# Attention stage of a one-core encoder trunk: TensorE's order written from a clock model, three block lanes, and two pieces of work given to GpSimd

## The chip, the core and the metric

The kernel runs on one core of one Trainium2 chip. The time is the device time of one execution in microseconds (us). The kernel before takes 3174.94 us, the median of three runs (3173.12 to 3175.65).

A core has five engines that run at the same time, each with its own queue of instructions in a fixed order. TensorE (PE in the profile; its weight loads are listed apart as PEld) multiplies matrices into the PSUM banks. VectorE (DVE) and ScalarE (ACT) read those banks and do the elementwise work. GpSimd (POOL) does elementwise work between SBUF tiles. SyncE (SP) issues most of the transfers.

## The reference, cut to what matters

The program is a trunk of two layers over 1024 positions of width 1024. Layer 0 mixes with two recurrent head groups and layer 1 with attention; each layer goes on with a squared-ReLU MLP and a gated embedding. The change is in the attention mixer of layer 1, 16 heads of width 64. Each chunk of 64 positions sees itself and the 8 chunks before it:

```python
qkv = (h @ w_qkv).reshape(bsz, seq, 3, C_HEADS, C_HEAD_DIM)
q = rmsnorm(qkv[:, :, 0], q_g) * (C_HEAD_DIM ** -0.5)
k = rmsnorm(qkv[:, :, 1], k_g)
v = qkv[:, :, 2]
...
s = jnp.einsum('bqhd,bkhd->bhqk', q_c, k_b).astype(jnp.float32) + bias
...
prob = jax.nn.softmax(s, -1).astype(v.dtype)
return jnp.einsum('bhqk,bkhd->bqhd', prob, v_b)
...
mix = chunk_band_attention(h, ...) @ attn_w_out[o]
x = x + mix
```

The bias is looked up by head and clipped relative distance.

## The kernel before

Positions lie in eight tiles of 128, and the 16 heads in 8 pairs. A matrix product in near-fp32 precision is made from three products of split operands (`mm3`, L305: high by high, high by low, low by high).

The attention stage is `layer1_in` (L1619). It has 16 steps, each a head pair `pr` and one half `hf` of the positions (four position tiles). A step has three parts, and a fourth piece of work stands beside them:

- **Input products**, `attn_in` (L1709): for each of the four position tiles 24 matmuls of 384 columns (q, k and v of two heads at once) into a bank with the tag `dense`; ScalarE copies q and k out, scaled (L1742), ScalarE and VectorE split v (L1746, L1747). Then the norms: GpSimd squares (L1754), VectorE sums (L1755), `rsqrt_small` (L280) makes 1/sqrt by three rounds of three small VectorE instructions (L287 to L289) and VectorE multiplies q and k by it (L1758, 128x1024). The weights of a pair are loaded by three transfers and split by ScalarE and VectorE (`load_qkv`, L1699, L1705, L1706).
- **Norm and layout**, `attn_norm` (L1761): four TensorE transposes for k and four for q into a `dense` bank; from there ScalarE writes the high parts (L1780), a second copy of the query at the other 64 partitions (L1782), and VectorE the low parts (L1783).
- **Four blocks** (two heads by two pairs of position tiles), `attn_block` (L1788): for each of its two tiles near scores into a bank `sn` and far scores into a bank `sf`; VectorE adds the bias table `toep` and takes the maximum in one instruction (L1838), ScalarE makes the exponentials (L1848, L1851) and scales by 1/sum (L1855). Then TensorE transposes the probabilities `pb` into banks `pt`, ScalarE and VectorE split them into `ptile` (L347, L348 in `split_scaled`), and TensorE multiplies by v into the bank `o` (`po`).
- **Filler**, the end of `attn_ins` (L1640): when the 16 steps' products are out, the products of the gated embedding (`ple_proj`, L1531) and the first part of the output projection (`out_early`, L1560).

PSUM has eight banks here: two `dense`, two `sn`, one `sf`, two `pt`, one `o`.

What sets the order. `run` (L128) is a small planner at build time: each part is a Python generator ("lane"), `self.now` is a time counted from the matmuls written so far (`mm` L165, `tr` L188), a lane that yields a name is not taken up again until `LAT[name]` microseconds later (a table, L35), one that yields a key waits until another lane has marked it, and the first lane in the list that is due is taken. Two lanes run `attn_block`, then come `attn_norms` and `attn_ins`. `attn_ins` may be three steps ahead of the finished ones (`("at", s - 3)`), `attn_norms` two. What the planner writes down is the program order. It isn't the final order: the whole program stands in

```python
with tile.TileContext(nc, schedule_with_timeline_sim=True) as tc:
```

so the framework's scheduler orders each engine's instructions anew, from the program order as a priority and a timeline that it simulates. The bias table of a head is prepared on GpSimd (L1796, L1797) in the head's first block.

Of the kernel before, what the change touches and what calls it, by code (L numbers as in the profile page):

```python
# [82 lines left out]
    "attn_norm0": 0.24,  # L83
    "attn_block0": 0.97,
    "attn_block1": 4.45,
    "attn_block2": 0.43,
    "attn_block3": 0.94,
    "qk": 11.25,
    "norm": 1.28,
# [17 lines left out]

class Trunk:
    def __init__(self, ctx, tc, a, dbg=None, stop=None):
        self.ctx, self.tc, self.nc, self.a = ctx, tc, tc.nc, a  # L110
        self.dbg, self.stop = dbg or {}, stop

        self.now, self.done, self.lat = 0.0, {}, LAT
        self.nd, self.rx, self.late, self.extra = -1, None, None, []

        self.steps, self.begun = [], None

# [10 lines left out]
    def run(self, lanes, ahead=()):  # L128
        state, self.done = [[g, 0.0, None] for g in lanes], {}
        ahead, self.steps = [lanes[n] for n in ahead], []  # L130
        waited = set()
        while state:
            best = None
            for st in state:
# [10 lines left out]
            self.begun, start = None, self.now  # L145
            try:
# [3 lines left out]
                continue  # L150
            if best[0] in ahead and self.begun is not None:
# [4 lines left out]
            if isinstance(r, tuple):  # L156
                best[2] = r
                waited.add(id(best[0]))
            else:
                best[1] = self.now + self.lat.get(r, 0.0)  # L160

    def mark(self, key, after=0.0):
        self.done[key] = self.now + after

    def mm(self, out, lhsT, rhs, start, stop):  # L165
# [5 lines left out]
        if rhs.dtype == F32:  # L171
# [16 lines left out]
    def tr(self, out, in_, ident):  # L188
        self.now += 0.107
# [90 lines left out]
    def rsqrt_small(self, out, x, shape, tag):  # L280
# [5 lines left out]
        for _ in range(3):  # L286
# [1244 lines left out]
    def ple_proj(self, i, pt, acc, scratch, sqt, load_w):  # L1531
# [9 lines left out]
        for n4 in range(2):  # L1541
            hi, lo = load_w(a["w_ple"][i, n4])
            for e in range(4):
                n = 4 * n4 + e
                t = scratch(n)
                for hf in range(2):
                    ps = self.bank()
# [12 lines left out]
    def out_early(self, i, xsrc, pair, xt, load_w, keys):  # L1560
# [36 lines left out]
        if i == 0:  # L1597
            raw = self.wr.tile([P, T], F32, tag="wraw", name="wraw")
            nc.sync.dma_start(out=raw, in_=a["w_out0"][2])
            self.w_next = self.split_w(raw, T, [self.pre.tile([P, T], F32R, tag=f"p{q}", name="w" + q) for q in "hl"])  # L1600
        self.first = [self.bank() for _ in ws]
# [17 lines left out]
    def layer1_in(self):  # L1619
        nc, tc, a = self.nc, self.tc, self.a  # L1620
        with ExitStack() as es:
# [16 lines left out]
            self.run([self.attn_lane(steps, jobs, l1, rbl) for _ in range(2)] + [self.attn_norms(steps, l1), self.attn_ins(steps, l1)])  # L1638

    def attn_ins(self, steps, l1):  # L1640
        kv = {}
        for s, (pr, hf) in enumerate(steps):
# [3 lines left out]
            self.mark(("qk", s), self.lat["qk"])  # L1646
# [29 lines left out]
    def attn_norms(self, steps, l1):  # L1676
        K = []
        for s, (pr, hf) in enumerate(steps):
            yield ("qk", s)
            if s >= 2:  # L1680
                yield ("at", s - 2)
            yield from self.attn_norm(s, self.st[s], l1)
# [3 lines left out]
            self.mark(("in", s), self.lat["norm"])  # L1686

    def attn_lane(self, steps, jobs, l1, rbl):

        for s, h, b in jobs:  # L1690
            yield ("in", s)
            yield from self.attn_block(s, *steps[s], h, b, l1, rbl)
# [16 lines left out]
    def attn_in(self, pr, hf, l1, kv):  # L1709
# [18 lines left out]
        for e in range(4):  # L1728
            i = 4 * hf + e
            ps = self.bank([P, 3, P])  # L1730
# [26 lines left out]
        self.rsqrt_small(nn, ss, [P, 16], "q")  # L1757
        V.tensor_tensor(q4, q4, nn.rearrange("p (n o) -> p n o", o=1).broadcast_to((P, 16, 64)), op=ALU.mult)  # L1758
        return dict(kv, qk=qk)

    def attn_norm(self, s, st, l1):  # L1761
# [5 lines left out]
        for j, g, nm in ((1, self.vec("kg"), "k"), (0, self.dv["qg8"], "Q")):  # L1767
            pt = self.bank()
# [10 lines left out]
            for h, r, o in ((0, h0, h1), (1, h1, h0)):  # L1779
                nc.scalar.activation(F[r, h], pt[r], AF.Copy, scale=g[r])  # L1780
                if not j:
                    nc.scalar.activation(F[o, h], pt[r], AF.Copy, scale=g[r])  # L1782
# [3 lines left out]
            yield "attn_norm0"  # L1786

    def attn_block(self, s, pr, hf, h, blk, l1, rbl):  # L1788
# [5 lines left out]
        if hf == 0 and blk == 0:  # L1794
            t = st["toep"][h]
            G.tensor_scalar(t, t, rbl[:, 2 * pr + h:2 * pr + h + 1], None, op0=ALU.subtract)  # L1796
# [201 lines left out]
```

## Time and profile before

| | |
|---|---|
| median of three runs | 3174.94 us (3173.12 to 3175.65) |
| the profiled execution | 3175.69 us, its span 3174.0 us |
| mean granted TensorE clock | 0.973 |
| input products of the stage, first and last matmul start | 1735.6 and 2255.1 us |
| last product into `po` starts | 2370.7 us |
| `toep` preparation on GpSimd, x16 | median 1297 ns |

The span runs from the first to the last instruction of the profiled execution; the execution's own time is 1.69 us more. The page gives the busy time of each engine, then groups of instructions: their line, engine, operation, what they write and read, how many, the busy time and the mean duration, and the idle time of the engine just before them with what ended it. The windows view gives busy times between two moments of the span, "(x...)" being numbers of instructions, then the granted TensorE clock and the transfers' share.

### The profile page before, as it was taken

To read this page: it belongs to the slowest core of one execution; us is meant where nothing else is said; L and a number is where in the kernel's file an instruction comes from. 1 tells how busy PE (TensorE), PEld (TensorE's weight loads), DVE (VectorE), ACT (ScalarE), POOL (GpSimd) and SP (SyncE) were. 2 spreads that over 40 slices of the span, in tenths; PEclk is the share of its full clock that TensorE was granted. 3 is DMA by queue.
4 is the path that set the end of the run, shared out by engine and by line. 5 is a ranking of instruction groups with operands and counts; after the bars stand their busy time and mean duration, and the time that the engine had idled before them with its cause. 6 is when DMAs were issued, how large, how long until landed. Compare 5 with 4: busy or idle time off the path is not lost.

```text
span 3174.0 us, 46034 instructions
## 1 busy us (share of the span) xinstructions
PE 3057.5 (96%) x17576; PEld 2523.9 (80%) x17576; DVE 2018.1 (64%) x4020; ACT 1387.8 (44%) x2640; POOL 536.1 (17%) x978
## 2 busy tenths in 40 slices
PE   7999999999999999999999989999999999999999
PEld 5777777777778888888887888888788888888887
DVE  6546666567849666655556576776769666655552
ACT  4323433333427554311223577777757555312221
POOL 6524443444500000000005111110200000000002
PEclk8989999999999999999999999999999999999999
DMA  3212112112345333522213100110255332522213
GB/s 128 77 48 64 50 43 85 54 57 64 126 153 209 136 120 112 190 93 100 99 54 129 58 32 33 47 39 16 76 197 205 136 120 107 199 93 93 107 47 106
DMA packets 144716, 309.60 MB, mean 98 GB/s; under 512 B 40944, under 2 KB 43120, under 8 KB 144496
## 3 DMA queue, kind: packets, MB, share of 16 engines
q1 hardware_dynamic: 126064, 273.10, 25.1%
q10 hardware_dynamic: 18432, 33.56, 2.7%
q8 instruction: 138, 2.26, 0.3%
q14 instruction: 82, 0.67, 0.1%
HBM read 232.16 MB, written 74.45 MB: 97 GB/s over the span
## 4 chain that ended last, share of the span: by engine, by line
PE 79%; DVE 10%; ACT 4%; DMA 4%; issue 2%; POOL 1%; SPq 0%; DVEq 0%; POOLq 0%; ACTq 0%
PE dps L175 67%; PE ch L175 2%; PE po L175 1%; PE pm L175 1%; PE iz L175 1%; PE tp L175 1%; DVE ptile L348 1%; PE pt L190 1%; DVE f L1056 1%; DMA wraw<-in_w_out 1%; PE sn L175 1%; DMA wraw<-in_w_qkv 1%; DVE wlo L302 1%; DVE pb L1838 1%; POOL subt L413 1%
## 5 line engine op out<-in xcount | busy, mean ns | idle before, releaser
L175 PE MATMUL dps<-r,act 128*128 128x512 f32 x3528 | 824.4, 392 | 0.0
L175 PEld LDWEIGHTS dps<-r,act 128*128 128x128 f32 x3528 | 662.2, 188 | 145.6
L175 PE MATMUL dps<-xg,whi 128*128 128x512 f32 x1280 | 437.9, 423 | 16.2 <-ACT xg L350 7.1
L175 PE MATMUL dps<-late,act 128*128 128x512 f32 x1536 | 352.9, 391 | 0.0
L175 PEld LDWEIGHTS dps<-late,act 128*128 128x128 f32 x1536 | 288.5, 188 | 63.1
L1495 POOL TENSOR_TENSOR pn<-pn,prs 128x512 f32<-128x512 f32 x32 | 47.1, 1475 | 1621.3 <-ACT prs L384 1527.3
L175 PE MATMUL dps<-wq,act 128*128 128x384 f32 x1536 | 304.8, 343 | 8.0 <-DVE vs L1747 4.2
L175 PEld LDWEIGHTS dps<-xg,whi 128*128 128x128 f32 x1280 | 237.2, 197 | 67.0 <-ACT xg L350 7.1
L175 PEld LDWEIGHTS dps<-wq,act 128*128 128x128 f32 x1536 | 264.5, 190 | 12.6 <-DVE vs L1747 7.0
L175 PE MATMUL dps<-xg,wlo 128*128 128x512 f32 x640 | 260.4, 408 | 2.0 <-DVE wlo L302 2.0
L1371 DVE TENSOR_TENSOR late<-late,dps 128x512 f32<-128x512 f32 x224 | 152.7, 684 | 152.4 <-PE dps L175 120.3
L1470 DVE TENSOR_TENSOR xw<-xw,dps 128x512 f32<-128x512 f32 x192 | 131.5, 685 | 154.6 <-PE dps L175 151.4
L1269 ACT CAST act<-act 128x1024 fp32r<-128x1024 f32 (+1 forms) x99 | 94.7, 963 | 282.9 <-DMA act<-in_w 119.4
L1269 ACT CAST act<-late 128x512 fp32r<-128x512 f32 x210 | 124.5, 618 | 139.5 <-PE dps L175 120.2
L1270 DVE TENSOR_TENSOR act<-late,act 128x512 fp32r<-128x512 f32 x210 | 139.7, 686 | 25.9 <-ACT act L1269 25.7
L175 PEld LDWEIGHTS dps<-xg,wlo 128*128 128x128 f32 x640 | 125.5, 196 | 33.2 <-DVE wlo L302 4.1
L301 ACT CAST whi<-wraw 128x1024 fp32r<-128x1024 f32 x78 | 81.7, 1048 | 152.7 <-PE dps L175 91.4
L175 PE MATMUL dps<-xw,act 128*128 128x512 f32 x576 | 138.9, 392 | 0.0
L175 PEld LDWEIGHTS dps<-xw,act 128*128 128x128 f32 x576 | 108.1, 188 | 24.1
L1270 DVE TENSOR_TENSOR act<-act 128x1024 fp32r<-128x1024 f32 (+1 forms) x99 | 109.9, 1114 | 18.3 <-ACT act L1269 17.2
L175 PE MATMUL po<-ptile,vs 128*128 128x256 f32 (+1 forms) x576 | 103.3, 293 | 17.5 <-DVE ptile L348 8.5
L302 DVE TENSOR_TENSOR wlo<-wraw,whi 128x1024 fp32r<-128x1024 f32 x78 | 99.3, 1274 | 27.5 <-ACT whi L301 27.1
(472 smaller groups left out, 5284.9 us busy)
## 6 DMA issues: line engine op xcount, KB each, us to landing
act<-in_w SPq DMA_DIRECT2D x68, 512.0 KB
hd<-late ACTq DMA_DIRECT2D x128, 256.0 KB
late<-in_w SPq DMA_DIRECT2D x60, 512.0 KB
wraw<-in_w_in SPq DMA_DIRECT2D x56, 512.0 KB
act<-hd SPq DMA_DIRECT2D x56, 512.0 KB
wraw<-in_w_out SPq DMA_DIRECT2D x21, 512.0 KB
wraw<-in_w_qkv SPq DMA_DIRECT2D x21, 512.0 KB
pn<-pnd SPq DMA_DIRECT2D x32, 256.0 KB
```

The costliest lines, as they stand in the source:

```text
L175: return self.begin(self.nc.tensor.matmul(out, lhsT, rhs, start=start, stop=stop))
L190: return self.begin(self.nc.tensor.transpose(out, in_, ident))
L301: nc.scalar.copy(hi, raw)
L302: nc.vector.tensor_tensor(lo, raw, hi.bitcast(F32), op=ALU.subtract)
L348: nc.vector.tensor_tensor(dst[:, 1, sl], src, dst[:, 0, sl].bitcast(F32), op=ALU.subtract)
L413: E.tensor_tensor(o, X[:, 0:i, i:i + 1].broadcast_to((NP, i, n)), Bq[:, i:i + 1, i + 1:16].broadcast_to((NP, i, n)), op=ALU.mult)
L1056: V.scalar_tensor_tensor(y, raws[j][:, i:i + HB], cw(i), y, op0=ALU.mult, op1=ALU.add)
L1269: A.copy(hi, s)
L1270: V.tensor_tensor(lo, s, hi.bitcast(F32), op=ALU.subtract)
L1371: V.tensor_tensor(r, t, u, op=ALU.add)
L1470: V.tensor_tensor(x[n][:, sl], x[n][:, sl], ps, op=ALU.add)
L1495: G.tensor_tensor(pn, pn, prs[:, sl], op=ALU.mult)
```

## The change

- A `Clock` follows every instruction as it is written: its engine, the regions of tiles it reads and writes, the bank or buffer that its tile takes, and a time by a formula per engine. Work on ScalarE, VectorE and GpSimd is placed in the first free gap of that engine after its operands are there; TensorE's time is `self.now`.
- The stage's planner now asks that clock. `when` says at which time operands are there for TensorE, `room` when a bank or buffer comes free, and `until` holds a lane back until then. The eight `attn...`, `qk` and `norm` entries of `LAT` are gone. Lanes have a priority: blocks by their number, `attn_norms` a little ahead of the blocks of its step, `attn_ins` last.
- TensorE's instructions of the stage are kept in the order in which they are written (`manual_schedule`); the other engines are still ordered by the scheduler.
- Three block lanes instead of two; `pb` has 6 buffers for 4, `mx` and `l` 8 for 4, `ptile` 4 for 3. The transposes of the blocks go in block order (`("tr", job - 1)`), then their products (`("pv", job - 1)`).
- On GpSimd: the rounds of `rsqrt_small` (twelve small instructions for the nine of VectorE; the first guess stays on VectorE), the multiplication of q and k by the norms, and the second copy of the query, from the first copy instead of from PSUM. The preparation of `toep` moves from the first block into `attn_norms`.

```diff
+class Clock:
+    HOP = {"PE": 0.2, "DMA": 0.1}
...
+    def time(self, e, ins, refs):
+        n = max([1] + [k for _, _, k in refs])
+        if e == "DMA":
+            return 2.2 + n * 0.0025
+        scalars = sum(not w and k == 1 for _, w, k in refs)
...
+        if e == "Activation":
+            return 0.15 + 0.00086 * n + 0.105 * (scalars > 0) + 0.19 * (sum(w for _, w, _ in refs) > 1)
+        if e == "DVE":
...
+            return 0.15 + 0.00105 * n + (0.06 if scalars and n > 16 else 0.0) + (0.08 if op == "ISA" else 0.0)
+        return 0.2 + 0.0021 * n
...
+    @contextmanager
+    def clock(self):
+        self.clk = Clock(self)
+        self.nc.push_inst_callback(self.clk.account)
+        with self.tc.manual_schedule(engines={mybir.EngineType.PE}):
+            yield
+        self.nc.pop_inst_callback()
+        self.clk = None
...
+    def until(self, f):
+        if self.clk:
+            yield f()
+            while f() > self.now + 0.02:
+                yield f()
...
     def run(self, lanes, ahead=()):
...
-                if st[1] <= self.now:
-                    best = st
-                    break
-                if best is None or st[1] < best[1]:
-                    best = st
+                key = max(st[1], self.now), st[3]
+                if best is None or key < first:
+                    best, first = st, key
...
+        if self.clk:
+            self.clk.dur = 2 * max(n / 1200, m * 0.00084) if rhs.dtype == F32 else max(n / 2260, m * 0.00084)
...
-    def rsqrt_small(self, out, x, shape, tag):
+    def rsqrt_small(self, out, x, shape, tag, G=None):
...
+        for _ in range(3 if G else 0):
+            G.tensor_tensor(w, out, out, op=ALU.mult)
+            G.tensor_tensor(w, w, x, op=ALU.mult)
+            G.tensor_scalar(w, w, -0.5, 1.5, op0=ALU.mult, op1=ALU.add)
+            G.tensor_tensor(out, out, w, op=ALU.mult)
...
     def dense_part(self, w, acts, evac, order=None):
...
+        yield from self.until(lambda: max(self.room("dense"), self.when(hi, lo, *[acts[k] for k in order])))
...
-            self.run([self.attn_lane(steps, jobs, l1, rbl) for _ in range(2)] + [self.attn_norms(steps, l1), self.attn_ins(steps, l1)])
+            with self.clock():
+                self.run([self.attn_lane(steps, jobs, l1) for _ in range(3)] + [self.attn_norms(steps, l1, rbl), self.attn_ins(steps, l1)])
...
     def attn_norms(...):
+            self.prio = 4 * s - 3
             yield ("qk", s)
             if s >= 2:
                 yield ("at", s - 2)
+            for h in range(0 if hf else 2):
+                t = self.st[s]["toep"][h]
+                self.nc.gpsimd.tensor_scalar(t, t, rbl[:, s + h:s + h + 1], None, op0=ALU.subtract)
+                self.nc.gpsimd.memset(t[0:64, 320:384], NEG)
             yield from self.attn_norm(s, self.st[s], l1)
...
     def attn_lane(self, steps, jobs, l1):
         for s, h, b in jobs:
+            self.prio = 4 * s + 2 * h + b
             yield ("in", s)
...
     def attn_in(...):
+            yield from self.until(lambda: max(self.room("dense"), self.when(wh, wl)))
             ps = self.bank([P, 3, P])
...
-        self.rsqrt_small(nn, ss, [P, 16], "q")
-        V.tensor_tensor(q4, q4, nn.rearrange(...), op=ALU.mult)
+        self.rsqrt_small(nn, ss, [P, 16], "q", G)
+        G.tensor_tensor(q4, q4, nn.rearrange(...), op=ALU.mult)
...
     def attn_norm(self, s, st, l1):
+            yield from self.until(lambda: max(self.room("dense"), self.when(qk)))
             pt = self.bank()
...
                 if not j:
-                    nc.scalar.activation(F[o, h], pt[r], AF.Copy, scale=g[r])
+                    nc.gpsimd.tensor_copy(F[o, h], F[r, h])
...
     def attn_block(...):
+            yield from self.until(lambda: self.room("sn", *(["sf"] if nf else [])))
             pn = psm.tile([P, HB], F32, tag="sn", name="sn", bufs=2)
...
-            yield "attn_block0"
-        yield "attn_block1"
+        yield self.when(*[pb for pb, _ in probs])
         job = 4 * s + 2 * h + blk
         if job:
-            yield ("pv", job - 1)
+            yield ("tr", job - 1)
...
         for b in range(bank + 1):
+            yield from self.until(lambda: max(self.room("pt"), self.when(*[pb for pb, _ in probs])))
             pt = psm.tile([P, HB], F32, tag="pt", name="pt", bufs=2)
...
+        self.mark(("tr", job))
+        if job:
+            yield ("pv", job - 1)
+        if blk == 0:
+            yield from self.until(lambda: self.room("o"))
+            st["po", h] = psm.tile([P, HB], F32, tag="o", name="po")
...
         for j, c0, c1 in segs:
+            if place[j][0] != b:
+                yield from self.until(lambda: self.when(pts[place[j][0]]))
```

More of the change, by code (lines that the diff above doesn't have):

```diff
@@ L1 @@
-from contextlib import ExitStack
+import bisect
+from contextlib import ExitStack, contextmanager
 import concourse.bass as bass
@@ L116, in __init__, with when, room @@
         self.steps, self.begun = [], None
+        self.clk = None
[6 more added lines that the diff above has]
+        self.nc.pop_inst_callback()
+        self.clk = None
+    def when(self, *aps):
+        if self.clk is None:
+            return 0.0
+        return max(self.clk.after(*self.clk.region(ap), "PE", False) for ap in aps)
+    def room(self, *tags):
+        if self.clk is None:
+            return 0.0
+        t = 0.0
+        for name in tags:
+            for tag in self.clk.bufs:
+                if tag.startswith(name + "_"):
+                    a = self.clk.acc.get(self.clk.next(tag), {})
+                    t = max([t] + [end + 0.2 for z, end in a.items()])
+        return t
+    def until(self, f):
[3 more added lines that the diff above has]
+                yield f()
     def dump(self, name, ap, idx=None):
@@ L128, in run @@
     def run(self, lanes, ahead=()):
-        state, self.done = [[g, 0.0, None] for g in lanes], {}
+        state, self.done = [[g, 0.0, None, 1000 * n + 1000] for n, g in enumerate(lanes)], {}
         ahead, self.steps = [lanes[n] for n in ahead], []
@@ L150, in run @@
                 continue
+            if self.prio is not None:
+                best[3] = self.prio
             if best[0] in ahead and self.begun is not None:
@@ L188, in tr @@
     def tr(self, out, in_, ident):
-        self.now += 0.107
+        if self.clk:
+            self.clk.dur = 0.109
+        else:
+            self.now += 0.107
         return self.begin(self.nc.tensor.transpose(out, in_, ident))
@@ L1546, in ple_proj @@
                 for hf in range(2):
+                    yield from self.until(lambda: max(self.room("dense"), self.when(hi, lo, pt(0, hf), pt(1, hf))))
                     ps = self.bank()
@@ L1600, in out_early @@
             self.w_next = self.split_w(raw, T, [self.pre.tile([P, T], F32R, tag=f"p{q}", name="w" + q) for q in "hl"])
+        yield from self.until(lambda: max(self.room("dense"), self.when(*[w for hl in ws for w in hl], *[y[k] for k in self.order[:6]])))
         self.first = [self.bank() for _ in ws]
@@ L1793, in attn_block @@
         m0 = 4 * hf + 2 * blk
-        if hf == 0 and blk == 0:
-            t = st["toep"][h]
-            G.tensor_scalar(t, t, rbl[:, 2 * pr + h:2 * pr + h + 1], None, op0=ALU.subtract)
-            G.memset(t[0:64, 320:384], NEG)
         hs = slice(64 * h, 64 * h + 64)
```

129 lines of the change are left out of this document (98 added, 31 removed).

## The prediction

> **What bounds the kernel now.** I read the page's busy times first, then the windows over the attention stage, then the groups of TensorE's weight loads in it.
>
> ```profile
> span 3174.0 us, 46034 instructions
> PE 3057.5 (96%) x17576; PEld 2523.9 (80%) x17576; DVE 2018.1 (64%) x4020; ACT 1387.8 (44%) x2640; POOL 536.1 (17%) x978
> ```
>
> TensorE is busy over 96% of the span, so only a stage in which it is less busy has anything to give. Windows (columns: the stretch, its length, busy us of PE, PEld, DVE, ACT and POOL with instruction counts, granted clock, transfer share, GB/s):
>
> ```profile
> 1780.00:2258.00 478.00, 438.65 (x2806) 412.86 (x2804) 337.50 (x1111) 352.01 (x833) 50.41 (x55) 0.99 0.10 35
> 2258.00:2386.00 128.00, 120.23 (x617) 100.53 (x618) 88.45 (x222) 82.64 (x172) 20.26 (x14) 0.96 0.50 175
> 1900.00:1920.00 20.00, 20.00 (x130) 19.93 (x130) 13.39 (x43) 15.81 (x37) 2.44 (x3) 0.95 0.06 18
> 1860.00:1880.00 20.00, 17.14 (x111) 15.75 (x112) 12.16 (x42) 15.57 (x39) 0.00 (x0) 1.00 0.04 14
> ```
>
> The first row is the body of the stage, where blocks and input products run together. Its matmul track is idle for 478.00 - 438.65 = 39.35 us, its weight-load track for 478.00 - 412.86 = 65.14 us (13.6%). The last two rows show that blocks and products can run with the loads at 99.7% (130 matmuls in 20 us), and that elsewhere the same mix gets 111 through. No other engine is near full: ACT 73.6%, DVE 70.6%, POOL 10.5%. What ends the loads' idle time (line, engine, operation, shapes, count, busy and mean ns of one, idle time before them and who ended it):
>
> ```profile
> L175 PEld LDWEIGHTS dps<-wq,act 128*128 128x128 f32 x1366 | 233.3, 189 | 8.9 <-DVE vs L1747 5.8 <-DVE F L1783 2.9
> L175 PEld LDWEIGHTS po<-ptile,vs 128*128 128x128 f32 x477 | 71.3, 197 | 24.2 <-DVE ptile L348 12.7 <-ACT ptile L347 11.0
> L190 PEld LDWEIGHTS pt<-ident,pb 128*128 128x128 f32 x401 | 47.8, 143 | 16.4 <-ACT pb L1855 9.0 <-DVE ptile L348 3.7 <-PE po L175 2.7
> L175 PEld LDWEIGHTS sn<-F,F 128*128 128x128 f32 x141 | 26.5, 189 | 4.1 <-DVE mx L1838 2.5 <-ACT F L1782 1.0
> L175 PEld LDWEIGHTS sf<-F,F 128*128 128x128 f32 x81 | 15.7, 194 | 6.4 <-ACT pb L1848 6.4
> L190 PEld LDWEIGHTS dps<-ident,qk 128*128 128x128 f32 x116 | 13.7, 140 | 4.5 <-DVE vs L1747 3.7
> ```
>
> These rows hold 64.5 of the 65.14 us. 51.1 us stand before block work (po, pt, sn, sf): TensorE reached a block's next step before VectorE or ScalarE had served it, with input products (the first row) standing behind it in the queue. 13.4 us (dps) are waits for the two dense banks. None is a wait for a transfer. So the order is what costs here.
>
> **The change, part by part.** The sum is made against the profiled execution, 3175.69 us, which is 0.75 us above the median.
>
> *Order and three lanes.* Nothing is added to TensorE; a step is written only when the clock says that its operands and bank are there, and products are written in the meantime. How good is the clock? It gives ScalarE 0.15 + 0.00086 x 384 + 0.105 + 0.19 = 0.775 us for an exponential of 384 with its sum, VectorE 0.15 + 0.00105 x 1024 = 1.225 us for the multiplication. The rows:
>
> ```profile
> L1851 ACT ACTIVATE pb<-pb,mx 128x384 f32<-128x384 f32 x81 | 49.5, 611 | 3.4 <-DVE mx L1850 3.4
> L1851 ACT ACTIVATION_READ_ACCUMULATOR pb<-pb,mx 128x1 f32 x109 | 21.0, 192 | 0.0
> L1855 ACT ACTIVATE pb<-pb,l 128x640 f32<-128x640 f32 x53 | 44.1, 832 | 11.6 <-DVE l L1854 9.8 <-DVE ss L1756 1.6
> L1758 DVE TENSOR_TENSOR qk<-qk,nn 128x1024 f32<-128x1024 f32 x14 | 17.1, 1222 | 0.3
> 1751.13 27.24 PE L175 MATMUL dps<-wq,act 128*128 128x384 f32 x144 [0.76 <-DVE ms L373]
> ```
>
> 0.803 and 1.222 us: the formulas are within 4%. A product takes 27.24 / 144 = 0.189 us against the clock's 384 / 2260 = 0.170: real TensorE is slower than the clock's, which makes operands early rather than late. What the clock lacks is the queue: it puts work into any free gap of ScalarE or VectorE, while the chip runs the scheduler's order. So some waits stay. The bounds: the loads stay at 412.86 / 478 = 86.4% (nothing), or run at 99.7% as in the best stretch (412.86 / 0.997 = 414.1, minus 63.9 us); below nothing is the first rival. I take the middle, 93%: 412.86 / 0.93 = 443.9, **minus 34 us**. Products can fill this: a step has 96 of them, 18.2 us.
>
> The Trainium skill (Perfetto Trace Analysis, Identifying the Most-Contended Engine) says that the busy share of matmuls misjudges the room on TensorE and that the share of weight loads is the better measure. By the matmul track the same middle (91.8% and 100%: 95.9%) gives 438.65 / 0.959 = 457.4, minus 21 us, and a time of 3152; no run so far decides between them.
>
> *Work given to GpSimd.*
>
> ```profile
> L1782 ACT ACTIVATE F<-dps,d_qg 64x512 fp32r<-64x512 f32 x30 | 20.5, 683 | 0.4
> L287 DVE TENSOR_TENSOR rsw<-nn 128x16 f32<-128x16 f32 x42 | 7.2, 171 | 0.6
> L288 DVE SCALAR_TENSOR_TENSOR rsw<-rsw,ss 128x16 f32<-128x16 f32 x42 | 7.8, 186 | 1.0
> L289 DVE SCALAR_TENSOR_TENSOR nn<-rsw,nn 128x16 f32<-128x16 f32 x42 | 7.2, 172 | 0.7
> L413 POOL TENSOR_TENSOR subt<-sub,subb 64x14 f32<-64x14 f32 x16 | 4.9, 306 | 1.2
> L695 POOL TENSOR_TENSOR wraw<-lraw,d_omul 128x1024 f32<-128x1024 f32 x2 | 3.9, 1954 | 2.8 <-DMA lraw<-in_lora 2.8
> L466 POOL COPY F<-X 32x256 f32<-32x256 f32 x32 | 18.0, 562 | 15.0 <-DVE X L453 13.7
> L1754 POOL TENSOR_TENSOR sq<-qk 128x512 f32<-128x512 f32 x29 | 30.2, 1041 | 368.6 <-ACT qk L1742 337.1 <-PE pt L190 16.9 <-DVE l L1854 14.7
> ```
>
> ScalarE is rid of 20.5 us, VectorE of 17.1 + 7.2 + 7.8 + 7.2 = 39.3 us of the body. On GpSimd, per step: 12 x 0.306 + 1.954 + two copies of 64x512 (between 0.562, fewer elements, and 1.041, as many elements and read twice; I take 1.041) = 7.7 us; 14.25 steps (1368 products by 96) make 110 us, with the 50.4 there 160 us, 36% of 444. That engine isn't full. But the chain from sum to normed q and k grows from 3 x 0.529 + 1.222 = 2.81 to 12 x 0.306 + 1.954 = 5.63 us, 2.8 us later per step. I cost it at nothing: the next step's products, 18.2 us, cover it, and they may be three steps ahead. Uncovered it is 16 x 2.8 = 45 us.
>
> The Trainium skill (GPSIMD Engine Reference, Engine selection) advises against GpSimd for elementwise work, as about twice slower than VectorE. In the rows here it is 1.954 to 1.222, 1.6 times; by the page's factor the multiplication would take 2.44 us, half a microsecond more under the same cover, and the sum would stay.
>
> *Bias table moved.* Two GpSimd instructions per head move ahead of the step's layout. Their transfer is issued where it was, and moves past no queue.
>
> ```profile
> POOL toep L1796 <- DMA toep<-in_rb: 47.0, 8, 8.9
> ```
>
> GpSimd waited 5.9 us on average for that transfer (8.9 at most), with nothing urgent behind it. Now the query copies and the next norms queue behind it. I cost that at nothing, under the same 18.2 us; without cover it is 7 pairs x 5.9 = 41 us.
>
> *The end of the stage*, 2258 to 2386:
>
> ```profile
> 2305.00:2310.00 5.00, 2.72 (x16) 2.38 (x15) 4.82 (x11) 3.28 (x6) 3.11 (x2) 0.82 0.43 120
> 2310.00:2315.00 5.00, 5.00 (x23) 4.56 (x22) 2.87 (x13) 3.21 (x7) 0.35 (x1) 0.50 0.64 231
> 2315.00:2320.00 5.00, 5.00 (x17) 3.96 (x16) 2.90 (x10) 3.13 (x8) 0.00 (x0) 0.65 0.99 307
> ```
>
> An idle 2.3 us is followed by a halved clock (0.18 + 0.50 + 0.35 of 5 us each, 5.2 us). Between 0 and minus 7 us if the order closes it; transfers are at 99% here, so I take **minus 2 us**. The stage's start waits for layer 0 and stays.
>
> Sum: 3175.69 - 34 - 2 = 3139.7; against the median, 3139.
>
> **Rivals.**
>
> *ScalarE sets the pace.* It is the busiest after TensorE, and its own waits don't go. At today's share, (352.01 - 20.5) / 0.736 = 450.4: minus 27.6, minus 2, 3146. For it: 15.57 of 20 us busy in the slack stretch above. Against: it reaches 15.81 in the tight one.
>
> *The pinned order is stale (slower).* A late operand now holds everything behind it, and the scheduler can't pull a ready product ahead. Place: the transposes of `pb`. If with three lanes ScalarE is one tile late for every block, each waits 0.611 + 0.192 + 0.832 = 1.635 us; today the loads idle 65.14 / 57 = 1.14 us per block (57 blocks in the body). 57 x 0.495 = 28 us more, 3203. It decides from 1.14 + 6.3 / 57 = 1.25 us per block. For it: 9.0 us before pt end on L1855 already. Against: the formulas' fit.
>
> *GpSimd decides when a step begins (slower).* Norms and table uncovered, 45 + 41 - 36 = 50 us more, 3225; from 42% of it exposed (36 of 86 us) the gain is gone. Against: 18.2 us of cover.
>
> *No change.* Only TensorE's order is pinned, the other queues keep their order and their lateness, and the waits move: 3169 to 3181.
>
> **Chances.** Forecast 0.48, ScalarE's pace 0.25, no change 0.10, stale order 0.11, GpSimd 0.06. A measurement of this kernel can tell about 0.2%, 6.3 us, from no change. Faster 0.73, same 0.10, slower 0.17. The range reaches from the best stretch kept up throughout, 3175 - 64 - 5 = 3106, to the end of no change, 3180; it leaves out the two slower rivals and little below.
>
> **What would show it.** Right: the stage shorter by some 36 us from its first product to the last into `po`, PEld at about 93% in its body, the idle before po and pt under half of 40.6 us, small L288 groups on POOL, none waited for by TensorE. Wrong: PEld below 86% in the body, long idle of PE before pt or po ended by L1855 or L348 (stale order), or PE idle before transposes of `qk` ended by POOL.

## The result, and the profile after

The changed kernel takes 3196.38 us (median of four runs, 3192.40 to 3196.92) against 3174.03 us for the kernel before on the same chip: a ratio of 1.0061, interval [1.0041, 1.0081]. It is slower by 22 us by the medians, by 19 us by the ratio. The forecast was 3139 us, 3106 to 3180. The sign was wrong and the time lies outside the range.

The profiled execution took 3196.31 us, its span is 3194.6 us. The head of the page:

```profile
span 3194.6 us, 46103 instructions
PE 3054.8 (96%) x17576; PEld 2528.8 (79%) x17576; DVE 1998.9 (63%) x3860; ACT 1366.8 (43%) x2608; POOL 628.7 (20%) x1218
```

TensorE has the same 17576 matmuls and is busy 3 us less in a span that is 20.6 us longer: the time came as idle time. To find where, the stage is cut from its first input product to the first product of the MLP after it (`dps<-act,late`), with the cuts at 1780 and 2258 that the prediction used for the body. The windows of before, then of after:

```profile
1735.57:1780.00 44.43, 35.91 (x191) 34.41 (x190) 20.37 (x44) 12.41 (x25) 16.12 (x17) 0.88 0.27 88
1780.00:2258.00 478.00, 438.65 (x2806) 412.86 (x2804) 337.50 (x1111) 352.01 (x833) 50.41 (x55) 0.99 0.10 35
2258.00:2383.48 125.48, 117.71 (x606) 98.48 (x607) 85.93 (x219) 80.28 (x168) 20.26 (x14) 0.96 0.49 172
```

```profile
1733.00:1780.00 47.00, 38.13 (x206) 36.40 (x205) 19.94 (x35) 13.78 (x26) 20.57 (x31) 0.89 0.24 81
1780.00:2258.00 478.00, 433.54 (x2826) 418.58 (x2825) 321.35 (x991) 335.02 (x818) 132.07 (x265) 0.96 0.10 33
2258.00:2400.78 142.78, 117.04 (x572) 95.59 (x571) 83.61 (x191) 74.73 (x153) 25.09 (x30) 0.94 0.45 151
```

The stage grew from 647.91 to 667.78 us, by 19.9 us, which is the span's growth but for 0.7 us. The idle time of PE (length minus busy) by part: start 8.5 and 8.9, body 39.4 and 44.5, end 7.8 and 25.7. That is 23.4 us more idle, less 3.6 us of shorter busy time: 19.9. Of the 23.4 us, 18.0 stand in the end of the stage, which the prediction's sum has with minus 2 us.

What ends the loads' idle time in the body of after (the groups that answer to those of the prediction):

```profile
L312 PEld LDWEIGHTS dps<-wq,act 128*128 128x128 f32 x1334 | 230.9, 193 | 6.1 <-issue 3.8 <-DVE F L1941 1.9 <-DVE vs L1904 0.4
L312 PEld LDWEIGHTS po<-ptile,vs 128*128 128x128 f32 x504 | 74.6, 203 | 7.9 <-DVE ptile L494 6.5 <-ACT ptile L493 1.4
L330 PEld LDWEIGHTS pt<-ident,pb 128*128 128x128 f32 x420 | 50.6, 145 | 19.4 <-ACT pb L2009 16.1 <-DVE ptile L494 1.8
L312 PEld LDWEIGHTS sn<-F,F 128*128 128x128 f32 x144 | 27.9, 194 | 0.0
L312 PEld LDWEIGHTS sf<-F,F 128*128 128x128 f32 x84 | 16.0, 191 | 2.3 <-ACT pb L2002 2.2
L330 PEld LDWEIGHTS dps<-ident,qk 128*128 128x128 f32 x112 | 12.4, 140 | 23.7 <-issue 8.6 <-POOL qk L1915 5.8 <-DVE vs L1904 4.2
```

The clock does part of what it promised: before po the idle fell from 24.2 to 7.9 us, before sn and sf from 10.5 to 2.3. But before the transposes of `qk`, which had 4.5 us, there are now 23.7, and before pt 19.4 for 16.4. In all, the loads' idle time in the body fell only from 65.1 to 59.4 us: most of the waits were not filled, they went to another place in the same order.

The row of the `qk` transposes puts 8.6 us down to "issue", which names nobody. The matmuls' rows of these transposes do name it (the whole stage, before and after):

```profile
L190 PE MATMUL dps<-ident,qk 128*128 128x128 f32 x128 | 19.9, 277 | 2.6 <-DVE vs L1747 2.4
L330 PE MATMUL dps<-ident,qk 128*128 128x128 f32 x128 | 20.7, 288 | 24.3 <-DVE F L1941 11.8 <-POOL qk L1915 8.8 <-DVE vs L1904 3.5
```

L1941 is VectorE's writing of the low parts, the last reader of the `dense` bank of earlier transposes; L1904 splits v out of the bank of an input product. So 15.3 of the 24.3 us are waits for a bank and 8.8 are waits for GpSimd: not only operands but banks too came free later than the clock said.

The end shows what a late instruction does to such an order. TensorE between 2264 and 2284 us, and the last lines of the stage (start, duration, what, idle time before it and who ended it):

```profile
2271.72 1.76 PE L312 MATMUL po<-ptile,vs 128*128 128x256 f32 x7 [2.05 <-DVE ptile L494]
2278.10 1.97 PE L330 MATMUL dps<-ident,qk 128*128 128x128 f32 x8 [4.62 <-POOL qk L1915]
2279.86 1.53 PE L330 MATMUL pt<-ident,pb 128*128 128x128 f32 x7
2283.02 1.16 PE L312 MATMUL dps<-act,wq 128*128 128x512 f32 x4 [1.63 <-DVE F L1941]
...
2337.05 58.45 PE L312 MATMUL dps<-act,wq 128*128 128x512 f32 x240
2400.78 1.22 PE L312 MATMUL dps<-act,late 128*128 128x512 f32 x2 [5.29 <-ACT late L1415]
```

The last input product has started at 2264.6. The norm of the last step isn't ready, its transposes stand next in TensorE's order, and the filler products (`dps<-act,wq`) are written behind them: they start at 2283.02. In the kernel before they started at 2258.63, three and a half microseconds after the last input product, and ran between the last blocks. Now 240 of them run alone at the very end, after the last block, where 54 did before. GpSimd in that hole:

```profile
2272.56 0.22 POOL L427 TENSOR_TENSOR rsw<-nn 128x16 f32<-128x16 f32 x1 [4.51 <-DVE nn L424]
...
2276.14 1.90 POOL L1915 TENSOR_TENSOR qk<-qk,nn 128x1024 f32<-128x1024 f32 x1
```

It starts only when VectorE has given the first guess, and takes 2276.14 + 1.90 - 2272.56 = 5.48 us. The idle time of the end is 11.4 us up to 2283, 4.2 from there to 2325 and 10.2 behind that. The last part holds the second new wait, 5.29 us ahead of the MLP's first product. It ends on a split of weights that were loaded late: the transfer of `in_w_out` was issued at 2395.53 us, right behind the stage's last product (2337.05 + 58.45 = 2395.50); in the kernel before it was issued at 2375.52, while that stage's products still ran.

### The profile page after: what moved, and what is told of

It is laid out like the page before. It is cut to its first block, busy times and chain, and to the rows that moved or that the text cites. A ratio compares the mean times of both kernels' runs of the same rounds, so it can differ in the third digit from the quotient of the medians.

```text
span 3194.6 us, 46103 instructions
## 1 busy us (share of the span) xinstructions
PE 3054.8 (96%) x17576; PEld 2528.8 (79%) x17576; DVE 1998.9 (63%) x3860; ACT 1366.8 (43%) x2608; POOL 628.7 (20%) x1218
## 4 chain that ended last, share of the span: by engine, by line
PE 79%; DVE 8%; ACT 5%; DMA 3%; POOL 3%; issue 2%; SPq 0%; ACTq 0%; POOLq 0%; DVEq 0%
PE dps L312 66%; PE ch L312 2%; PE po L312 2%; PE pm L312 1%; PE pt L330 1%; PE iz L312 1%; PE tp L312 1%; PE sn L312 1%; DVE f L1202 1%; ACT pb L2009 1%; POOL subt L559 1%; ACT pb L2005 1%; DVE wlo L447 1%; POOL sub L561 1%; DMA wraw<-in_w_qkv 1%
## 5 line engine op out<-in xcount | busy, mean ns | idle before, releaser
L1416 DVE TENSOR_TENSOR act<-late,act 128x512 fp32r<-128x512 f32 x210 | 139.9, 687 | 27.7 <-ACT act L1415 27.6
L1416 DVE TENSOR_TENSOR act<-act 128x1024 fp32r<-128x1024 f32 (+1 forms) x99 | 110.1, 1115 | 23.4 <-ACT act L1415 22.6
L1521 ACT ACTIVATE late<-late 128x512 f32<-128x512 f32 x128 | 80.2, 629 | 85.3 <-DVE late L1517 84.0
```

What stands on the lines that cost most here:

```text
L1416: V.tensor_tensor(lo, s, hi.bitcast(F32), op=ALU.subtract)
L1521: A.activation(t, t, AF.Relu)
```

## The experiments

Theory 1: the order that TensorE now has to keep is what costs; a late operand holds everything behind it. Theory 2: the work on GpSimd comes too late for TensorE. Theory 3: the larger buffers push a weight buffer to a place where the MLP's weights must wait for it, and only the end of the stage loses. The kernel before had a median of 3175.90 us beside the first four experiments, 3177.14 beside the next four, and 3174.79 beside the last three. Each ratio is to the kernel before measured beside it.

### The order written, but not enforced

```diff
-        with self.tc.manual_schedule(engines={mybir.EngineType.PE}):
-            yield
+        yield
```

> The kernel after, but TensorE's order in the stage is left to the scheduler again; the clock, the three lanes and the GpSimd work stay. Theory 1 (the pinned order is stale: a late operand holds everything behind it): TensorE takes ready products first, the idle time of the weight loads before the transposes of qk and pb (29.8 and 27.6 us over the stage after the change) falls to about 5 and 18 us as before, and about 20 us are given back: 3170 to 3180. Theory 2 (GpSimd's longer chain is late whatever the order): the waits stay, 3190 to 3200. Theory 3 (only the end of the stage lost): 3190 to 3200 with the 5.3 us wait for the tail's first weights still there.

Measured: 3174.43 us, ratio 0.9993 [0.9979, 1.0007]. The whole loss is gone by this alone: 1.0061 - 0.9993 = 0.68%, 21.6 us. Its windows, cut in the same way:

```profile
1731.40:1780.00 48.60, 37.02 (x200) 35.16 (x199) 20.10 (x37) 13.98 (x27) 21.29 (x32) 0.89 0.23 78
1780.00:2258.00 478.00, 446.46 (x2870) 431.14 (x2868) 320.94 (x1024) 344.03 (x845) 133.42 (x265) 0.96 0.11 36
2258.00:2378.07 120.07, 108.15 (x536) 90.67 (x535) 74.93 (x157) 63.98 (x125) 24.96 (x29) 0.94 0.50 171
```

PE idle: 11.6 in the start, 31.5 in the body, 11.9 in the end. Against the pinned kernel the body has 12.9 us less and the end 13.8 less. The groups of its body:

```profile
L311 PEld LDWEIGHTS po<-ptile,vs 128*128 128x128 f32 x504 | 76.9, 198 | 19.2 <-ACT ptile L492 8.9 <-DVE ptile L493 6.7 <-ACT F L1937 1.6
L329 PEld LDWEIGHTS pt<-ident,pb 128*128 128x128 f32 x423 | 52.9, 148 | 11.8 <-ACT pb L2008 4.9 <-issue 2.8 <-DVE ptile L493 1.6
L329 PEld LDWEIGHTS dps<-ident,qk 128*128 128x128 f32 x112 | 13.7, 150 | 6.5 <-POOL qk L1914 3.9 <-DVE F L1940 1.0 <-POOL sq L1910 0.7
```

The transposes of `qk` wait 6.5 us for the pinned kernel's 23.7, with the same GpSimd work ahead of them. Theory 1 holds as far as this: the pin is what cost. Two things qualify it. Without the pin VectorE and ScalarE are ordered otherwise too: of VectorE's 1230 instructions in the stage, the longest sequence that both kernels have in the same order holds 755 (the pinned kernel and the one of the third experiment share 1218). So TensorE's order isn't separated from what the pin does to the other queues. And the late filler isn't the pin's alone: here too it starts some 18 us after the last input product (2251.8 and 2269.5), 195 of its matmuls run alone behind the last block, and 5.2 us of idle time stand ahead of the MLP.

### The norms and the copy back on VectorE and ScalarE, order still pinned

```diff
-        self.rsqrt_small(nn, ss, [P, 16], "q", G)
-        G.tensor_tensor(q4, q4, nn.rearrange("p (n o) -> p n o", o=1).broadcast_to((P, 16, 64)), op=ALU.mult)
+        self.rsqrt_small(nn, ss, [P, 16], "q")
+        V.tensor_tensor(q4, q4, nn.rearrange("p (n o) -> p n o", o=1).broadcast_to((P, 16, 64)), op=ALU.mult)
...
-                    nc.gpsimd.tensor_copy(F[o, h], F[r, h])
+                    nc.scalar.activation(F[o, h], pt[r], AF.Copy, scale=g[r])
```

> The kernel after, but the rounds of the norm, the multiplication by it and the second query copy are back on VectorE and ScalarE; the pinned order, the clock and the three lanes stay. Theory 2 (GpSimd's chain decides): the 29.8 us of idle weight loads before the transposes of qk fall to about 8 us and the slow clock goes with them, 3165 to 3175. Theory 1 (stale order): VectorE and ScalarE are fuller, the same waits come back before pt and po, 3190 to 3205.

Measured: 3274.52 us, 1.0297 [1.0275, 1.0320]. Both theories missed, by 70 us and by 100, and theory 2 has the sign wrong as well: without the GpSimd work the pinned kernel is 2.36%, 75 us, slower still. The loads' groups over the whole stage:

```profile
L312 PEld LDWEIGHTS dps<-wq,act 128*128 128x128 f32 x1536 | 281.2, 201 | 38.4 <-issue 30.6 <-PE pt L330 4.8 <-ACT act L496 1.1
L330 PEld LDWEIGHTS pt<-ident,pb 128*128 128x128 f32 x480 | 60.7, 150 | 28.1 <-ACT pb L2009 23.5 <-DVE ptile L494 2.5
L330 PEld LDWEIGHTS dps<-ident,qk 128*128 128x128 f32 x128 | 18.6, 171 | 37.4 <-DVE qk L1915 30.8 <-ACT pb L2009 2.7 <-issue 2.1
```

The transposes of `qk` now wait 30.8 us for VectorE's multiplication. It takes less time there than on GpSimd but is served later. Which work VectorE does ahead of it was not taken apart. Their whole wait grew only from 29.8 to 37.4 us, though; before the input products it grew from 8.2 to 38.4, nearly all of it "issue". The matmuls' row names what that is, VectorE's low parts again, which hold the bank:

```profile
L312 PE MATMUL dps<-wq,act 128*128 128x384 f32 x1536 | 312.1, 355 | 34.0 <-DVE F L1941 32.5 <-ACT act L496 0.8 <-DVE ms L519 0.5
```

And 22 us are no idle time at all: TensorE's busy time in the stage is 610.8 us against 588.7 in the change, at a granted clock of 0.88 in the body against 0.96. (The clock plans anew at build time, so the pinned order is not the same one.)

### The buffer of `pb` moved in SBUF

```diff
+            self.wpb = es.enter_context(self.pool("l1b", 2))
...
-            pb = self.wp.tile([P, 5 * P], F32, tag="pb", name="pb", bufs=6)
+            pb = self.wpb.tile([P, 5 * P], F32, tag="pb", name="pb", bufs=6)
```

Two more `pb` and one more `ptile` buffer make the stage's pool larger and push the pool of its second weight buffer, opened behind it, to higher addresses, under the place that the MLP's weights take; this is argued from the order of the pools, no run shows the addresses. Here `pb` gets a pool of its own, opened behind that weight buffer.

> The kernel after, but the buffers of pb lie in a pool of their own behind the pool of the stage's second weight buffer, so that this buffer lies where it lay before the change. Theory 3 (larger buffers pushed that weight buffer under the first weight buffer of the tail, whose load then waits for the stage's last product): the 5.3 us of TensorE before the tail's first product and the half clock behind it go, 6 to 9 us less, 3187 to 3190. If the place isn't the cause: 3196, with the wait.

Measured: 3190.11 us, 1.0044 [1.0030, 1.0059]. TensorE at the end of the stage:

```profile
2340.40 58.34 PE L312 MATMUL dps<-act,wq 128*128 128x512 f32 x240
2398.58 3.66 PE L312 MATMUL dps<-act,late 128*128 128x512 f32 x15
```

The 5.29 us ahead of the MLP's first product are gone: the transfer of `in_w_out` is issued at 2389.63 us, while the products run. The time lies just above the 3187 to 3190 of theory 3. The two ratios differ by 0.17%, 5 us; their intervals overlap, so the trace is the better evidence: the wait came from where the buffers lie.

### The kernel before with the GpSimd work alone

The edits of the norms and the copy as in the change (`rsqrt_small` with the rounds on GpSimd that the change's diff shows), in the kernel before, with its two lanes and its own planner.

```diff
-        self.rsqrt_small(nn, ss, [P, 16], "q")
-        V.tensor_tensor(q4, q4, nn.rearrange("p (n o) -> p n o", o=1).broadcast_to((P, 16, 64)), op=ALU.mult)
+        self.rsqrt_small(nn, ss, [P, 16], "q", G)
+        G.tensor_tensor(q4, q4, nn.rearrange("p (n o) -> p n o", o=1).broadcast_to((P, 16, 64)), op=ALU.mult)
...
-                    nc.scalar.activation(F[o, h], pt[r], AF.Copy, scale=g[r])
+                    nc.gpsimd.tensor_copy(F[o, h], F[r, h])
```

> The kernel before with only the GpSimd part of the change: the rounds of the norm, the multiplication by it and the second query copy on GpSimd; two lanes, the old planner, the scheduler's order. Theory 2 (GpSimd's chain is late for the transposes of qk): slower by 10 to 20 us, 3185 to 3195, with idle time before these transposes. Theory 1 (only the pinned order makes it late): within 5 us of 3174, or a few us faster since ScalarE loses 22 us and VectorE 44 us of work.

Measured: 3175.90 us, 1.0002 [0.9986, 1.0018]. No change. Theory 2 falls: the longer chain costs nothing where the scheduler may order TensorE, and taking nearly 40 us of work from VectorE brings nothing either.

### The kernel before with its own order pinned

```diff
-            self.run([self.attn_lane(steps, jobs, l1, rbl) for _ in range(2)] + [self.attn_norms(steps, l1), self.attn_ins(steps, l1)])
+            with self.tc.manual_schedule(engines={mybir.EngineType.PE}):
+                self.run([self.attn_lane(steps, jobs, l1, rbl) for _ in range(2)] + [self.attn_norms(steps, l1), self.attn_ins(steps, l1)])
```

> The kernel before with one thing of the change: TensorE's instructions of the stage are kept in the order in which the old planner writes them. Theory 1 (a written order is late against the chip, and pinning it is what costs): slower by 20 us or more, above 3195, with more idle weight loads before the transposes of pb and the products into po than the 18.5 and 27.1 us of the kernel before. Rival (the clock's order is what is bad, pinning is harmless): within 6 us of 3175.

Measured: 3260.46 us, 1.0268 [1.0248, 1.0287], 85 us slower. The loads' groups over the stage:

```profile
L175 PEld LDWEIGHTS dps<-wq,act 128*128 128x128 f32 x1536 | 274.8, 199 | 26.6 <-issue 13.3 <-DVE vs L1748 11.2 <-ACT act L350 0.9
L175 PEld LDWEIGHTS sf<-F,F 128*128 128x128 f32 x96 | 18.4, 192 | 37.7 <-ACT pb L1849 37.6
L190 PEld LDWEIGHTS dps<-ident,qk 128*128 128x128 f32 x128 | 16.1, 155 | 40.1 <-issue 32.7 <-DVE vs L1748 3.3 <-ACT sq L1554 2.3
```

The sign is the one of theory 1, the place isn't: before pt and po the loads wait 15.4 and 14.7 us, less than the 18.5 and 27.1 of the kernel before. The waits grew before sf (8.9 to 37.7, its one bank held until ScalarE's exponential), before the transposes of `qk` (5.1 to 40.1) and before the products. The matmuls' rows say what the "issue" is, a `dense` bank until VectorE has written low parts:

```profile
L175 PE MATMUL dps<-wq,act 128*128 128x384 f32 x1536 | 331.5, 358 | 23.1 <-DVE Ql L1784 12.1 <-DVE vs L1748 9.6 <-ACT act L350 0.5
L190 PE MATMUL dps<-ident,qk 128*128 128x128 f32 x128 | 23.0, 309 | 34.4 <-DVE F L1784 29.3 <-DVE vs L1748 2.4 <-ACT sq L1554 1.5
```

So in the kernel before, leaving TensorE's order to the scheduler is worth 85 us. The change as a whole loses 22 us by its pin. That isn't the clock's merit alone: pinned and without the GpSimd work the clock's order, with its three lanes, stands at 1.0297, no better than the old planner's 1.0268 here, and its pin costs 75 us (1.0060 without it, two experiments below). The loss is small only with the clock's order and the GpSimd work together. The old planner's order was not pinned together with the GpSimd work, so how much the clock itself brings to a pinned order stays open.

### Order not enforced, and the buffer moved

The edits of the first and the third experiment together:

```diff
-        with self.tc.manual_schedule(engines={mybir.EngineType.PE}):
-            yield
+        yield
...
+            self.wpb = es.enter_context(self.pool("l1b", 2))
```

> The kernel after, unpinned as in the first experiment, and with the buffers of pb in a pool of their own so that the second weight buffer lies where it lay before. Theory 3: the two effects add, the 5.6 us wait before the tail's first product goes and the half clock behind it, 3174 less 6 to 9, 3165 to 3168, a little faster than the kernel before. If the scheduler's order moves with the place: 3170 to 3178.

Measured: 3169.61 us, 0.9980 [0.9967, 0.9992]: the only version faster than the kernel before, by 0.2%, about what a measurement tells from nothing. It lies between the two ranges expected. Its body:

```profile
1780.00:2258.00 478.00, 445.37 (x2859) 430.44 (x2857) 318.74 (x1004) 339.91 (x833) 133.75 (x266) 0.95 0.10 33
```

The loads are at 90.1%, a little over half the way from 86.4 to the forecast 93.

### Order not enforced, norms and copy back on VectorE and ScalarE

The edits of the first and the second experiment together:

```diff
-        with self.tc.manual_schedule(engines={mybir.EngineType.PE}):
-            yield
+        yield
...
-        self.rsqrt_small(nn, ss, [P, 16], "q", G)
+        self.rsqrt_small(nn, ss, [P, 16], "q")
```

> The kernel after, unpinned, and with the norms and the query copy back on VectorE and ScalarE: of the change only the clock's program order and the three lanes are left. The pinned kernel without GpSimd took 3274.5. Theory 1 (a pinned order can't follow a fuller VectorE, the scheduler's can): 3170 to 3185, about 95 us less than pinned. Rival (VectorE's own queue was too full with three lanes, whatever TensorE does): 3230 or more.

Measured: 3195.43 us, 1.0060 [1.0044, 1.0077], 21 us above the first experiment. It lies between the two ranges expected, 10 us above the one of theory 1. Loads before po over the stage:

```profile
L311 PEld LDWEIGHTS po<-ptile,vs 128*128 128x128 f32 x576 | 89.8, 205 | 29.7 <-ACT ptile L492 15.0 <-DVE ptile L493 9.3 <-DVE y L2054 2.7
```

In the first experiment this group had 21.7 us over the stage. So the GpSimd work is worth nothing in the kernel before, 21 us in the clock's program order, and 75 us where that order is pinned. Why the freed time of VectorE and ScalarE counts in the clock's program order and not in the old one isn't shown.

### The kernel before with three lanes

Three lanes, and the larger buffers with `pb` in the pool of the third experiment, under the old planner.

```diff
+            self.wpb = es.enter_context(self.pool("l1b", 2))
...
-            self.run([self.attn_lane(steps, jobs, l1, rbl) for _ in range(2)] + [self.attn_norms(steps, l1), self.attn_ins(steps, l1)])
+            self.run([self.attn_lane(steps, jobs, l1, rbl) for _ in range(3)] + [self.attn_norms(steps, l1), self.attn_ins(steps, l1)])
...
-            mx = sm.tile([P, 4], F32, tag="mx", name="mx", bufs=4)
-            pb = self.wp.tile([P, 5 * P], F32, tag="pb", name="pb", bufs=4)
+            mx = sm.tile([P, 4], F32, tag="mx", name="mx", bufs=8)
+            pb = self.wpb.tile([P, 5 * P], F32, tag="pb", name="pb", bufs=6)
```

In this kernel a head's second or a later block can read its bias table before GpSimd has prepared it, so some scores carry the unprepared table. The next experiment has the table in order.

> The kernel before with three block lanes and the larger buffers of the change (pb in its own pool, so that the second weight buffer stays where it was), the old planner and the scheduler's order. If a third lane gives the scheduler earlier scores to choose from: faster by 5 to 20 us. If the scheduler orders by its own timeline and two blocks in flight were enough: within 6 us of 3175.

Measured: 3193.79 us, ratio 1.0043 [1.0028, 1.0058]. Slower, where both expectations had it faster or unchanged.

### Three lanes, the bias table prepared in `attn_norms`

The same, and the preparation of `toep` where the change has it.

```diff
+            for h in range(0 if hf else 2):
+                t = self.st[s]["toep"][h]
+                self.nc.gpsimd.tensor_scalar(t, t, rbl[:, s + h:s + h + 1], None, op0=ALU.subtract)
+                self.nc.gpsimd.memset(t[0:64, 320:384], NEG)
...
-        if hf == 0 and blk == 0:
-            t = st["toep"][h]
-            G.tensor_scalar(t, t, rbl[:, 2 * pr + h:2 * pr + h + 1], None, op0=ALU.subtract)
-            G.memset(t[0:64, 320:384], NEG)
```

> The kernel before with three block lanes and the larger buffers (pb in its own pool), and with the bias table prepared in the norms' lane as in the change, so that no block can come before its table. Old planner, the scheduler's order. If the third lane itself costs under the old planner: 3185 to 3200 as in the run without the moved table. If that run's order of the table was what cost: within 6 us of 3177.

Measured: 3183.23 us, 1.0027 [1.0016, 1.0037]. It lies just below the range of the one theory and just above the other's. Under the old planner a third lane, with its larger buffers and the moved table, costs 8 us. Its loads over the stage:

```profile
L175 PEld LDWEIGHTS sf<-F,F 128*128 128x128 f32 x96 | 18.6, 193 | 12.6 <-ACT pb L1849 12.3
```

The kernel before has 8.9 us there. This fits the single `sf` bank, held until ScalarE's exponential, which one lane more asks for; it is 3.7 of the 8 us.

### The clock's order without enforcement, with two lanes

The kernel that was faster (order not enforced, buffer moved), with one lane less:

```diff
-                self.run([self.attn_lane(steps, jobs, l1) for _ in range(3)] + [self.attn_norms(steps, l1, rbl), self.attn_ins(steps, l1)])
+                self.run([self.attn_lane(steps, jobs, l1) for _ in range(2)] + [self.attn_norms(steps, l1, rbl), self.attn_ins(steps, l1)])
```

> The fastest kernel so far (after, unpinned, weight buffer in its old place, 3169.6) with two block lanes instead of three. If the clock's order needs the third lane to keep products and blocks apart: 3175 to 3190. If two blocks in flight are enough once GpSimd has the norms: 3163 to 3172.

Measured: 3176.81 us, 1.0008 [0.9996, 1.0019]. The third lane is worth 0.28%, 9 us, in the clock's program order; the intervals of the two kernels don't overlap. So a third lane costs 8 us under the one planner and brings 9 under the other. With two lanes the clock's order and the GpSimd work together bring nothing that can be measured.

### The transposes of `qk` written 4 us later, order pinned

```diff
-            yield from self.until(lambda: max(self.room("dense"), self.when(qk)))
+            yield from self.until(lambda: max(self.room("dense"), self.when(qk) + 4.0))
```

> The kernel after, pinned, but the planner takes the normed q and k for 4 us later than its clock says before it writes their transposes. Theory 1 in its narrow form (the written order is stale at this one place, since GpSimd's chain ends later than the clock believes): the 29.8 us of idle weight loads before the transposes of qk fall below 12 us and the time by 10 to 20 us, 3176 to 3187. Rival (lateness only moves: the steps begin later and the blocks run out of work): the waits go to pt, po or the products, 3195 to 3215.

Measured: 3222.21 us, 1.0149 [1.0136, 1.0162], 0.88% (28 us) slower than the change. The loads' groups over the stage:

```profile
L312 PEld LDWEIGHTS dps<-wq,act 128*128 128x128 f32 x1536 | 267.8, 193 | 18.2 <-issue 11.1 <-DVE vs L1904 4.8 <-ACT act L496 1.2
L312 PEld LDWEIGHTS po<-ptile,vs 128*128 128x128 f32 x576 | 86.2, 205 | 25.7 <-DVE ptile L494 14.9 <-ACT ptile L493 8.0 <-DVE y L2055 1.6
L330 PEld LDWEIGHTS pt<-ident,pb 128*128 128x128 f32 x480 | 59.1, 149 | 39.8 <-ACT pb L2009 27.8 <-DVE ptile L494 6.9 <-issue 2.4
L330 PEld LDWEIGHTS dps<-ident,qk 128*128 128x128 f32 x128 | 15.2, 145 | 6.3 <-issue 2.8 <-ACT act L1701 2.0 <-PE dps L312 1.3
```

The margin does remove the wait it was meant for, 6.3 us over the stage where the change has 29.8. What is late then is the blocks: pt and po together have 65.5 us, against 39.6 in the change (27.6 and 12.0), and the input products 18.2 against 8.2. So lateness moved to the next steps, as the rival said, and by 7 us more than its range; this margin at one place was no cure.

## Why the prediction was wrong, point by point

- **What bounds the kernel: the rows were read rightly, the conclusion is not shown.** 51 us of idle time stood before block work. "So the order is what costs here" would need an order that wins them back; the best version gains 0.2%. The count was off as well: 57 blocks in the body come from the input products, the 477 of 576 loads into `po` make it 53, so 1.23 us of idle loads per block and not 1.14.
- **Order and three lanes, minus 34 us: this step failed.** "I take the middle, 93%": the loads reached 418.58 / 478 = 87.6% pinned. The step took a *written* order for a denser one. Its own caveat ("the chip runs the scheduler's order") was priced as some waits that stay; the pinned order in fact gives up the scheduler's reordering, which pinning the old order puts at 85 us and unpinning the new one at 22 us. In place of minus 34 us, the body's idle time went from 39.4 to 44.5 us and the stage grew by 19.9. "Products can fill this" failed for the same reason: products are there, but behind the late instruction, as the hole at 2264 to 2283 us shows. "Real TensorE is slower than the clock's, which makes operands early" didn't hold at the transposes of `qk` and `pb`: 23.7 and 19.4 us in the body, the first mostly for banks. And the formulas fit less well than "within 4%": a product is 0.170 us in the clock and 0.189 in the trace, and GpSimd's multiplication 0.2 + 0.0021 x 1024 = 2.35 us against 1.905.
- **The middle was not reached without the pin either, and 99.7% by no run.** Without the pin the body does reach 431.14 / 478 = 90.2%, and even then the stage is only 1.2 us shorter (646.67 to 647.91), since the start has 3.1 us and the end 4.2 us more idle time. A body is not a stage.
- **Work given to GpSimd, at nothing: right for the kernel before, wrong for this one.** The chain was forecast at 5.63 us and is 5.48. Alone in the kernel before it costs and brings nothing. In the clock's order it brings 21 to 75 us, which I had nowhere. "Uncovered it is 45 us" was a price for a loss that isn't there; the waits for POOL that did appear (10.6 us before the transposes of `qk`) belong to the pin: unpinned, all their waits are 7.5 us over the stage.
- **Bias table moved, at nothing: not tested against the pin.** In the trace of the change VectorE, which reads the tables, has no idle time that ends on their preparation, and the one GpSimd instruction that waits behind a table waits 5.1 us, as before (5.2). Under three lanes and the old planner its move made the time 0.16% less, with intervals that overlap.
- **End of the stage, minus 2 us: wrong sign,** 125.48 to 142.78 us. I looked at an idle stretch and the halved clock that follows it, and not at what fills the stage once the input products are out. The pin costs as much there as in the whole body: 13.8 and 12.9 us of idle time that the first experiment removes (the start gives 2.7 back). The 5 us of the weights' late transfer were a cost of the larger buffers, which I had taken to be free.
- **The rivals.** The stale order was forecast at 3203 us; 3196.38 came. Its mechanism is the one found, and its place half so: before pt there are 9 us more over the stage, before the transposes of `qk` 25. Its point of decision was wrong: the body has 478 - 418.58 = 59.42 us of idle loads for 56 blocks (504 of the 576 loads into `po`, 64 blocks), 1.06 us each, below the 1.25 from which it was to decide. I had tied it to the blocks alone. GpSimd as the one that decides is refuted by both kernels that take its work back, which are slower; ScalarE's pace and "no change" did not come, though without the pin "no change" would have been the result.
- **Chances.** 0.11 on the stale order was too little for a change whose one certain effect is to take a freedom away. What spoke "against" it was the fit of the clock's formulas; durations that fit within 4% don't give the place of an instruction in the queue of ScalarE, VectorE or GpSimd, and the trace of before cannot show an order that wasn't run.
- **The signs.** "PEld below 86% in the body" did not come (87.6%). The idle before po and pt was to fall under half of 40.6 us; it fell to 27.3. The idle before pt ended by the scaling of `pb` and the idle before the transposes of `qk` ended by POOL both did. The share of the loads rose by 1.2 points while the matmuls' fell from 91.8% to 90.7% and the stage grew. The Trainium skill (Perfetto Trace Analysis, Identifying the Most-Contended Engine) prefers the loads' share as the measure of room; here neither share of the body told of the end. Over the whole stage both fell, the loads' from 84.2% to 82.4% and the matmuls' from 91.4% to 88.2%.

What stays open: why the clock's program order needs the GpSimd work so much, why 19.2 us before po remain in the body when nothing is enforced, and how much of the pin's cost is TensorE's order and how much the other queues'.

## What to carry to other kernels

Before an engine's order is pinned, ask what the scheduler now does with it, and run both: keep the new program order as a priority first (the first experiment is one line), and pin only what then still waits. A plan's times for operands and banks must hold for the queues of all engines, not only for durations; a late operand or bank in a pinned queue holds all that stands behind it. And larger buffers weren't free here: look at which later transfer waits for the space that they push aside.

## What was not expected of the hardware

GpSimd's instructions in the body of after (count, busy us and mean ns of one, idle time before them):

```profile
L1915 POOL TENSOR_TENSOR qk<-qk,nn 128x1024 f32<-128x1024 f32 x14 | 26.7, 1905 | 0.9
L1940 POOL CAST F<-F 64x512 fp32r<-64x512 f32 x29 | 17.7, 610 | 63.4 <-ACT F L1938 60.8 <-DVE F L1941 1.2 <-DVE y L2055 1.2
L430 POOL TENSOR_TENSOR nn<-nn,rsw 128x16 f32<-128x16 f32 x42 | 11.3, 269 | 3.5
```

A copy of 64x512 took 0.61 us where I had taken 1.04 from a two-input instruction, so GpSimd was busy 132.07 of 478 us, 28% and not 36%. The multiplication of 128x1024 took 1.905 us against VectorE's 1.222, 1.56 times. The granted clock in the body was 0.99 before, 0.96 in the change and 0.88 in the second experiment. The waits alone don't tell why: the first experiment idles less there than the kernel before (31.5 against 39.4 us) and has 0.96, and the old order pinned idles nearly as much as the second experiment (76.9 against 82.5 us) and has 0.94.
